# A fused decoder block: first group's values split between the exponentials, and a gate copied out of PSUM by two engines

## The chip, the cores and the metric

The kernel runs on one core of a Trainium2 chip. Five engines work side by side, each on its own list of instructions in a fixed order: PE (matrix multiplication; it reads SBUF and writes PSUM), DVE (vector), ACT (scalar functions and copies), POOL, and SP, which here only issues transfers (DMAs). POOL issues transfers too, on a queue of its own. Semaphores connect the lists: an instruction that waits holds up everything behind it on its engine. The metric is the device time of one execution in microseconds (us). Times of events below are counted from the start of the span.

## The reference

The reference is a whole decoder block over 1024 tokens and 1024 channels in float32: normalization, a chunked retention branch, a dilated-attention branch, sigmoid gates that merge the two, and an MLP. What matters here is the attention branch and its gate:

```python
s = einsum(q, k) * dh**-0.5 + bias
mx = max(s); e = exp(s - mx); den = sum(e)      # per query
p = e / den; lse = mx + log(den)
o = einsum(p, v)
...
wts = softmax(stack(lses))                       # over the 3 groups
att = einsum('gbhs,gbhsd->bshd', wts, o_all)
merged = sigmoid(gate_a) * ret_out + sigmoid(gate_b) * att_out
```

There are three groups of four heads with different windows and dilations. The softmax over the groups mixes the outputs of the groups, head by head.

## The kernel before, in words

Every matrix product is done as three passes: each float32 operand is split into a high part (a rounded copy, made by ACT) and a low part (the rest, made by DVE as `x - hi`), and PE adds low times high, high times low and high times high (`mm3`, L197 to L205).

The program is a list of steps written out by hand. `Steps.run` (L72) goes through it: before a step's body it prepares the weights of the next one or two steps. A weight arrives by one SP transfer of 512 KB into one of three `raw` buffers (L85); `split_w` (L188) makes `raw…h` on ACT and `raw…l` on DVE. As a buffer is used up, the next load is issued on SP.

The attention runs in two passes over pairs of heads (`pair` 0 and 1). The order in a pair is `combos` (L1470): groups 1, 2 and 0, two heads `a` each. Step `att_step(pair, i)` (L1472) projects the keys of `combos[i]` on PE (tile `ak`), and between these matmuls PE computes the scores of `combos[i-1]` (tiles `sc`). DVE adds the bias (tile `P`), takes the row maximum and its negative (`ng`); ACT does the exponentials in place (`scores_end`, L1256). When both heads of group 1 or 2 are done, `stats_out` (L1325) writes their maxima and sums to DRAM (`std`) and reads them back in the order of the tokens (`stn`): two SP transfers, where the second waits for the first to land.

Then come the cover steps (`cover_step`, L1507), which carry one gate projection each on PE (tile `gate`, in one of two PSUM buffers of two banks), as cover for the attention's tail:

- n = 0 computes the scores of the last head of group 0, its exponentials, then `weights(pair)` (L1333): a short chain DVE, ACT (exponential of `wt`, L1346), DVE, which gives the weight of each group. `pscale(0, a)` then scales the probabilities of group 0, blocks shared by DVE (L1367) and ACT (L1369). Only then does ACT do the sigmoid of the first gate out of PSUM (L1538; a table of functions is loaded first), and SP writes it to DRAM.
- n = 1 computes the second gate, and in its middle splits the values of group 0 (`v_split(pair, 0)`, L1297: `vh` on ACT, `vl` on DVE).
- n = 2 begins the products of probabilities and values (`pv`): PE transposes blocks of `P` into PSUM (`pt`, L1384), ACT and DVE split them (`pth` L1388, `ptl` L1389), PE multiplies them with `vl` and `vh` (L1408 to L1410). Between these PE computes the third gate, which takes the PSUM buffer of the first.

The values lie in DRAM (`va_d`). `v_fetch(pair, g)` (L1291) loads them by two SP transfers of 512 KB, cut in rows of 256 numbers (1 KB). For group 0 this is issued at the start of the last key step (`i == len(combos) - 1`). On the list of SP these transfers come after `std` and `stn` of group 2 and after the weight loads of the third and fourth gates.

At the end of the retention, `result_sums` (L574) gives POOL four sums of 2 MB blocks in DRAM, each a copy followed by an accumulating transfer (`dma_sum`, L566 and L567), each of these waiting for the one before it. They run on POOL's queue while the attention of pair 0 begins.

Of the kernel before, what the change touches and what calls it, by code (L numbers as in the profile page):

```python
# [11 lines left out]
F32 = mybir.dt.float32  # L12
F32R = mybir.dt.float32r
AF = mybir.ActivationFunctionType
# [120 lines left out]
def block_kernel(ctx, tc, io, stop=None, dbg=None):  # L135
    nc = tc.nc
    ctx.enter_context(tc.manual_schedule())

    def fv(t):
        return t.bitcast(F32)  # L140
# [350 lines left out]
    def at(gen, n, call):  # L491

        for i, _ in enumerate(gen):
            if i == n:
                call()
            yield

    def drain(gen):
        for _ in gen:
            pass  # L500
# [458 lines left out]
    gate_d = [dram.tile([P, S], F32, name=f"gated{i}") for i in range(16)]  # L959
# [165 lines left out]
    A = {}  # L1125
# [9 lines left out]
    def ring(name, dt=F32R):  # L1135
        return A["p"].tile([P, 1024], dt, tag="ring", bufs=8, name=name)
# [3 lines left out]
    def pslice(g, t, blk):  # L1140

        if g == 0:
            return (t[:, 0:128], 1) if blk == 0 else (t[:, 128 + 256 * (blk - 1):128 + 256 * blk], 2)
        if g == 1:
            r, n = blk // 2, blk % 2
            return (t[:, 384 * r:384 * r + 128], 1) if n == 0 else (t[:, 384 * r + 128:384 * r + 384], 2)
        return t[:, 128 * blk:128 * (blk + 1)], 1
# [108 lines left out]
    def scores_end(pair, g, a):  # L1256
        p, t, st = A["p"], A["P", g, a], A["st"]
        if g == 0:
            nc.vector.reduce_max(st[:, g, 0:1, a], t[:, 0:128], axis=AX.X)
            nc.vector.reduce_max(st[:, g, 1:8, a], t[:, 128:].rearrange("p (b x) -> p b x", b=7), axis=AX.X)  # L1260
        elif g == 1:
            tv = t.rearrange("p (r x) -> p r x", r=4)
            sv = st[:, g].rearrange("p (r n) x -> p r n x", n=2)
            nc.vector.reduce_max(sv[:, :, 0, a], tv[:, :, 0:128], axis=AX.X)
            nc.vector.reduce_max(sv[:, :, 1, a], tv[:, :, 128:384], axis=AX.X)
        else:
            nc.vector.reduce_max(st[:, g, :, a], t.rearrange("p (b x) -> p b x", b=8), axis=AX.X)
        ng = p.tile([P, 8], F32, tag="ng", bufs=2, name=f"ng{pair}{g}{a}")
        nc.vector.tensor_scalar_mul(ng, st[:, g, :, a], -1.0)  # L1269
        for blk in range(8):  # L1270
            v = pslice(g, t, blk)[0]
            nc.scalar.activation(v, v, AF.Exp, bias=ng[:, blk:blk + 1], accum_out=st[:, g, blk, 2 + a:3 + a])  # L1272
# [13 lines left out]
    def v_tile(pair, g, j, n):  # L1286
        if g == 0:
            return A["r1"].tile([P, S], F32R, tag="att", bufs=8, name=f"{n}{pair}{g}{j}")
        return ring(f"{n}{pair}{g}{j}")
# [4 lines left out]
            lo = A["l", g, j] = v_tile(pair, g, j, "vl")  # L1294
            nc.sync.dma_start(fv(lo).rearrange("p (a b) -> p a b", a=4), v_rows(pair, g, j))

    def v_split(pair, g):  # L1297
        for j in range(2):
            lo = A["l", g, j]
            hi = v_tile(pair, g, j, "vh")  # L1300
            nc.scalar.copy(hi, fv(lo))
            nc.vector.tensor_sub(lo, fv(lo), fv(hi))
            A["v", g, j] = (hi, lo)

    def vblk(g, blk, a, i):
        j, b = (blk % 2, blk // 2) if g == 1 else (blk // 4, blk % 4)
# [14 lines left out]
    def blocks(t, g):  # L1321

        return t.rearrange("p (r n) x -> p r n x", n=2) if g == 1 else t
# [9 lines left out]
    def weights(pair):  # L1333

        p, st = A["p"], A["st"]
        stn = [st[:, 0], A["stn"][:, 1], A["stn"][:, 2]]
        mx = p.tile([P, 8, 2], F32, tag="mx", name=f"mx{pair}")
        wt = p.tile([P, 3, 8, 2], F32, tag="wt", name=f"wt{pair}")
        pr = p.tile([P, 3, 8, 2], F32, tag="pr", name=f"pr{pair}")
        sm = p.tile([P, 8, 2], F32, tag="ssum", name=f"ssum{pair}")  # L1340
        wg = p.tile([P, 2, 8, 2], F32, tag="wg", name=f"wg{pair}")
        nc.vector.tensor_max(mx, stn[0][:, :, 0:2], stn[1][:, :, 0:2])
        nc.vector.tensor_max(mx, mx, stn[2][:, :, 0:2])
        for g in range(3):
            nc.vector.tensor_sub(wt[:, g], stn[g][:, :, 0:2], mx)
        nc.scalar.activation(wt, wt, AF.Exp)  # L1346
        for g in range(3):
            nc.vector.tensor_mul(pr[:, g], wt[:, g], stn[g][:, :, 2:4])
        nc.vector.tensor_add(sm, pr[:, 0], pr[:, 1])
        nc.vector.tensor_add(sm, sm, pr[:, 2])  # L1350
        nc.vector.reciprocal(sm, sm)
        for g in range(3):
            nc.vector.tensor_mul(wt[:, g], wt[:, g], sm)
        A["w", 0] = wt[:, 0]
        ds = [dram.tile([S, 2], F32, name=f"wtd{pair}{g}") for g in (1, 2)]
        for g in (1, 2):
            nc.sync.dma_start(natural(ds[g - 1], 0, 2), wt[:, g])
        for g in (1, 2):
            nc.sync.dma_start(blocks(wg[:, g - 1], g), natural(ds[g - 1], g, 2))
            A["w", g] = wg[:, g - 1]  # L1360

    def pscale(g, a):
        t, w = A["P", g, a], A["w", g]
        for blk in range(8):
            v = pslice(g, t, blk)[0]
            if blk in (0, 2, 4, 5, 7):
                nc.vector.tensor_scalar_mul(v, v, w[:, blk, a:a + 1])  # L1367
            else:
                nc.scalar.mul(v, v, w[:, blk, a:a + 1])  # L1369
        A["scaled", g, a] = True  # L1370
# [85 lines left out]
    def weave_pv(main, n, pair, *groups):  # L1456


        parts, waits = sum(4 * len(PT[g]) for g in groups), 2 * len(groups) + 1
        heavy = max(1.0, (parts - waits) / max(1, n - waits))  # L1460
        total = parts + waits * (heavy - 1)
        done = share = 0
        for wait in pv(pair, *groups):
            share += heavy if wait else 1
            while done * total < share * n:
                next(main, None)
                done += 1
        drain(main)

    combos = [(g, a) for g in (1, 2, 0) for a in range(2)]  # L1470

    def att_step(pair, i):  # L1472

        g, a = combos[i]

        def body(*args):
            ps = ps_mm(f"ak{pair}{i}")
            gen = proj_gen(ps, args[-1])
            if i == len(combos) - 1:
                v_fetch(pair, 0)  # L1480
            if i > 0:
                last = combos[i - 1]
                weave(gen, NK, scores_gen(pair, *last), len(SB[last[0]]), lag=2)
            elif pair == 0:
                args[0](1, True)
                for _ in range(4):
                    next(gen)
                on_T(H - 1, NC - 1)
                drain(gen)
                u_final(H - 1)  # L1490
                result_sums()
                open_att()
                args[0](3)
            else:

                weave_pv(at(gen, 0, lambda: v_split(0, 2)), NK - 1, 0, 2)
            if i == 0:
                A["st"] = A["p"].tile([P, 3, 8, 4], F32, tag="st", name=f"st{pair}")
                bias_load(pair)
            k_split(pair, g, a, ps)  # L1500
            if i > 0:
                scores_end(pair, *last)
                if last[1] == 1:
                    stats_out(pair, last[0])
        return body

    def cover_step(pair, n):  # L1507


        i = COVER[pair][n]  # L1510

        def body(*args):
            ps = ps_mm(f"gate0{i}")
            gen = proj_gen(ps, args[-1])
            if n == 0:
                v_fetch(pair, 1)
                weave(gen, 6, scores_gen(pair, *combos[-1]), len(SB[0]), lag=2, rest=False)
                drain(gen)
                scores_end(pair, *combos[-1])
                weights(pair)  # L1520
                for a in range(2):
                    pscale(0, a)
            elif n == 1:
                drain(at(gen, 4, lambda: v_split(pair, 0)))
            elif n == 2:
                v_fetch(pair, 2)

                gen = at(gen, 3, lambda: (args[0](3), v_split(pair, 1)))
                weave_pv(gen, NK - 1, pair, 0)
                for a in range(2):  # L1530
                    pscale(1, a)
            else:
                weave_pv(at(gen, 3, lambda: [pscale(2, a) for a in range(2)]), NK - 1, pair, 1)
            if n > 1:
                t = A["r1"].tile([P, S], F32, tag="att", bufs=8, name=f"g0{i}s")
            else:
                t = ring(f"g0{i}s", F32)
            nc.scalar.activation(t, flat(ps), AF.Sigmoid)  # L1538
            nc.sync.dma_start(gate_d[i], t)
        return body  # L1540

    for pair in range(2):
# [916 lines left out]
```

## Time and profile before

| | |
|---|---|
| median of 3 runs | 2226.19 us (2223.69 to 2228.32) |
| the profiled execution | 2226.56 us, of which the span is 2224.8 us |
| PE busy | 2177.1 us, 98% of the span |
| DVE, ACT, POOL busy | 65%, 41%, 7% of the span |
| transfers | 408.93 MB, mean 184 GB/s |

In the rows of a timeline the first two columns are the start and the busy time in us (of all instructions merged in the row), then engine, line, operation, the tile written and those read, the shape and the count. In brackets stands how long the engine had been idle before it and what ended that. Rows of waits give the engine and line that waited, what for, the total in us, how many times, and the longest. Rows of the transfer queues give packets, MB, and the time that the packets took, as a share of sixteen transfer engines. POOL's queue is `q0 software_dynamic`, SP's is `q1 hardware_dynamic`.

### The profile page before, as it was taken

The numbers are of one execution on the slowest core, as the hardware profiler recorded it, in microseconds if no ns is written. First come the engines' busy times: TensorE is split into PE (matmuls) and PEld (weight loads), VectorE is DVE, ScalarE is ACT, GpSimd is POOL, SyncE is SP. The second block draws the span as 40 slices with busy tenths as digits, with TensorE's granted clock in tenths as the row PEclk, the third lists the DMA queues.
The fourth block names the chain that finished last, engine by engine and source line by source line (L and its number), as shares of the span: only waits on it lengthen the run. The fifth ranks groups of instructions, "written<-read, shape, count | busy, mean of one in ns | idle before, by whom it ended". The sixth has DMA issues, their size and how long they took to land.

```text
span 2224.8 us, 27161 instructions
## 1 busy us (share of the span) xinstructions
PE 2177.1 (98%) x10130; PEld 1803.4 (81%) x10130; DVE 1454.5 (65%) x2285; ACT 907.3 (41%) x1665; POOL 145.5 (7%) x168
## 2 busy tenths in 40 slices
PE   7999999999999999999999999999999999999998
PEld 4888888888877888888888788888778888888887
DVE  6628777764448778855554644676876665787855
ACT  4323332223434445544534633424454445533412
POOL 0001111000012122100000000002100000000003
PEclk9999999999999999999999999999999999999999
DMA  9539999725775556549813355645144444745322
GB/s 364 200 134 284 299 284 284 200 103 189 250 268 169 167 179 212 188 162 248 235 60 96 105 196 211 237 160 176 62 149 152 149 156 168 261 139 171 122 85 77
DMA packets 154371, 408.93 MB, mean 184 GB/s; under 512 B 27062, under 2 KB 54973, under 8 KB 149822
## 3 DMA queue, kind: packets, MB, share of 16 engines
q1 hardware_dynamic: 148542, 363.14, 46.5%
q0 software_dynamic: 5696, 44.04, 8.4%
q8 instruction: 80, 1.31, 0.2%
q14 instruction: 53, 0.43, 0.1%
HBM read 316.27 MB, written 156.13 MB: 212 GB/s over the span
## 4 chain that ended last, share of the span: by engine, by line
PE 86%; DVE 6%; ACT 3%; DMA 2%; issue 1%; POOL 0%; SPq 0%; POOLq 0%; DVEq 0%; ACTq 0%
PE qap L203 5%; PE qap L201 5%; PE qap L205 5%; PE av L769 4%; PE fp L203 4%; PE fp L201 4%; PE fp L205 4%; PE rg L201 2%; PE rg L203 2%; PE rg L205 2%; PE f2a L203 2%; PE f2a L201 2%; PE f2a L205 2%; PE ak L201 2%; PE ak L203 2%; PE ak L205 2%
## 5 line engine op out<-in xcount | busy, mean ns | idle before, releaser
L201 PE MATMUL qap<-hh,qaw 128*128 128x512 f32 x216 | 84.0, 389 | 0.0
L203 PE MATMUL qap<-hl,qaw 128*128 128x512 f32 x216 | 84.0, 389 | 0.0
L205 PE MATMUL qap<-hh,qaw 128*128 128x512 f32 x216 | 84.0, 389 | 0.0
L616 POOL TENSOR_TENSOR j<-qk,j 128x512 fp32r<-128x512 f32 x32 | 43.3, 1352 | 465.0 <-ACT j L615 465.0
L1918 ACT ACTIVATE a<-a 128x512 f32<-128x512 f32 x48 | 30.3, 632 | 76.2 <-DVE a L1917 76.2
L1272 ACT ACTIVATE P<-P,ng 128x128 f32<-128x128 f32 (+1 forms) x96 | 41.9, 438 | 39.2 <-DVE ng L1269 39.2
L258 DVE TENSOR_TENSOR fw<-w1r,fw 128x512 fp32r<-128x512 f32 x48 | 33.0, 688 | 37.6 <-ACT fw L248 37.6
L1815 POOL TENSOR_TENSOR accnf<-accnf,sqnf 128x256 f32<-128x256 f32 (+1 forms) x18 | 16.6, 922 | 613.5 <-ACT sqnf L1814 613.4
L258 DVE TENSOR_TENSOR qaw<-wa,qaw 128x512 fp32r<-128x512 f32 x54 | 36.0, 685 | 30.9 <-ACT qaw L248 30.9
L2104 ACT CAST w2h<-w2s 128x512 fp32r<-128x512 f32 x36 | 22.4, 621 | 78.1 <-DVE w2s L2142 77.0
L201 PE MATMUL fp<-h2h,fw 128*128 128x512 f32 x128 | 50.0, 390 | 0.0
L203 PE MATMUL fp<-h2l,fw 128*128 128x512 f32 x128 | 49.8, 389 | 0.0
L205 PE MATMUL fp<-h2h,fw 128*128 128x512 f32 x128 | 49.8, 389 | 0.0
L201 PE MATMUL roa<-rh,rwl 128*128 128x512 f32 x128 | 49.8, 389 | 0.0
L203 PE MATMUL roa<-rl,rwh 128*128 128x512 f32 x128 | 49.8, 389 | 0.0
L205 PE MATMUL roa<-rh,rwh 128*128 128x512 f32 x128 | 49.8, 389 | 0.0
L1653 DVE TENSOR_TENSOR rwl<-rwl,rwh 128x1024 fp32r<-128x1024 f32 x25 | 30.2, 1221 | 29.1 <-ACT rwh L1683 29.1
L638 ACT COPY sm<-sT 128x128 f32<-128x128 f32 x32 | 8.5, 266 | 98.8 <-PE sT L629 92.7
L201 PEld LDWEIGHTS qap<-hh,qaw 128*128 128x128 f32 x216 | 40.5, 188 | 8.5
L205 PEld LDWEIGHTS qap<-hh,qaw 128*128 128x128 f32 x216 | 40.5, 188 | 8.4
L203 PEld LDWEIGHTS qap<-hl,qaw 128*128 128x128 f32 x216 | 40.5, 188 | 8.4
L1815 POOL TENSOR_TENSOR accn<-accn,sqn 128x512 f32<-128x512 f32 x12 | 15.5, 1294 | 478.5 <-ACT sqn L1814 478.5
(3081 smaller groups left out, 7181.0 us busy)
## 6 DMA issues: line engine op xcount, KB each, us to landing
v<-vd SPq DMA_DIRECT2D x32, 512.0 KB, 4.9
raw<-in_w_ada_dram SPq DMA_DIRECT2D x32, 512.0 KB, 4.9
w1r<-in_w_ff_dram SPq DMA_DIRECT2D x32, 512.0 KB, 5.0
vd<-vo SPq DMA_DIRECT2D x24, 512.0 KB, 6.5
yt<-y POOLq DMA_DIRECT2D x6, 2048.0 KB, 15.3
xsd<-as SPq DMA_DIRECT2D x24, 512.0 KB, 2.7
w2r<-in_w_ff2s_dram SPq DMA_DIRECT2D x24, 512.0 KB, 7.6
em<-in_w_ada_dram SPq DMA_DIRECT2D x16, 512.0 KB, 10.2
```

Source lines behind the costliest of these rows:

```text
L201: nc.tensor.matmul(o, wl, xh, start=first, stop=False, skip_group_check=skip)
L203: nc.tensor.matmul(o, wh, xl, start=False, stop=False, skip_group_check=skip)
L205: nc.tensor.matmul(o, wh, xh, start=False, stop=last, skip_group_check=skip)
L258: nc.vector.tensor_sub(t[:, 512:], src, fv(t[:, :512]))
L616: nc.gpsimd.tensor_sub(t[:, 1], src, fv(t[:, 0]))
L638: nc.scalar.copy(sm, ps[:, :C])
L769: nc.tensor.matmul(av[g][c], x[k][:, c * C:(c + 1) * C], w[j][:, ws], start=k == 0 and (x, j) == parts[0], stop=k == NK - 1 and (x, j) == ...
L1272: nc.scalar.activation(v, v, AF.Exp, bias=ng[:, blk:blk + 1], accum_out=st[:, g, blk, 2 + a:3 + a])
L1653: nc.vector.tensor_sub(lo, fv(lo), fv(hi))
L1815: (nc.vector if f == 7 else nc.gpsimd).tensor_add(G["acc", key], G["acc", key], sq)
L1918: nc.scalar.activation(o, o, AF.Relu)
L2104: nc.scalar.copy(hi, src)
```

## The change

The change has these parts, for each of the two pairs:

1. `v_fetch(pair, 0)` is issued one key step earlier (`len(combos) - 2`). On SP's list its two transfers now stand ahead of `std` and `stn` of group 2 and of the loads of the third and fourth gates.
2. The high parts `vh` of group 0 are made on ACT in step n = 0, between the exponentials of the two heads of group 0, instead of in step n = 1.
3. The low parts `vl` are made on DVE inside `weights`, while ACT does the last exponentials and that of `wt`.
4. The first gate is copied out of PSUM after `pscale`: its first half by DVE, its second by ACT. Its sigmoid is done in place in step n = 1, after that of the second gate, and so is its write to DRAM; the table load moves with it.

```diff
-    def v_split(pair, g):
+    def v_split(pair, g, low=True):
         for j in range(2):
             lo = A["l", g, j]
             hi = v_tile(pair, g, j, "vh")
             nc.scalar.copy(hi, fv(lo))
-            nc.vector.tensor_sub(lo, fv(lo), fv(hi))
             A["v", g, j] = (hi, lo)
+            if low:
+                v_low_part(g, j)
+
+    def v_low_part(g, j):
+        hi, lo = A["v", g, j]
+        nc.vector.tensor_sub(lo, fv(lo), fv(hi))
...
         nc.scalar.activation(wt, wt, AF.Exp)
+
+        for j in range(2):
+            v_low_part(0, j)
...
-            if i == len(combos) - 1:
+            if i == len(combos) - 2:
                 v_fetch(pair, 0)
...
                 drain(gen)
+                v_split(pair, 0, False)
                 scores_end(pair, *combos[-1])
                 weights(pair)
                 for a in range(2):
                     pscale(0, a)
+
+                t = ring(f"g0{i}s", F32)
+                nc.vector.tensor_copy(t[:, :512], ps[:, 0])
+                nc.scalar.copy(t[:, 512:], ps[:, 1])
             elif n == 1:
-                drain(at(gen, 4, lambda: v_split(pair, 0)))
+                drain(gen)
...
+            if n == 0:
+                A["gate"] = i, t
+                return
...
             nc.scalar.activation(t, flat(ps), AF.Sigmoid)
             nc.sync.dma_start(gate_d[i], t)
+            if n == 1:
+                i0, t0 = A["gate"]
+                nc.scalar.activation(t0, t0, AF.Sigmoid)
+                nc.sync.dma_start(gate_d[i0], t0)
```

## The prediction

> **What bounds the kernel now.** I read the page first, then the waits and the timeline of PE around the changed steps, then ACT and DVE in the same stretch, and last SP's list, the transfer queues and POOL.
>
> ```profile
> span 2224.8 us, 27161 instructions
> PE 2177.1 (98%) x10130; PEld 1803.4 (81%) x10130; DVE 1454.5 (65%) x2285; ACT 907.3 (41%) x1665; POOL 145.5 (7%) x168
> ```
>
> PE is busy for all but 48 us of the span, and the matmuls are the same after the change. So only PE's idle gaps count, those that close and those that open. Pair 0, PE:
>
> ```profile
> 1079.51 0.60 PE L1384 MATMUL pt000(0, 0, 0)_8939<-ct,P 128*128 128x128 f32 x4
> 1080.89 0.73 PE L201 MATMUL gate<-hh,raw_8603l 128*128 128x512 f32 x2 [0.79 <-ACT g00s L1538]
> 1085.96 0.38 PE L1409 MATMUL pv<-ptl000(0, 0, 0)_8945,vh 128*128 128x256 f32 x1 [0.45 <-DVE ptl000(0, 0, 0)_8945 L1389]
> ```
>
> Pair 1, from the waits of PE:
>
> ```profile
> PE gate L201 <- ACT g04s L1538: 0.8, 1, 0.8
> PE pv L1409 <- DVE ptl100(0, 0, 0)_10284 L1389: 0.5, 1, 0.5
> ```
>
> The third gate waits until ACT has emptied the first gate's PSUM buffer, and the first value products wait until DVE has the low part of the transposed probabilities. Pair 1 repeats pair 0. Behind these waits stand ACT and DVE:
>
> ```profile
> 1063.52 1.03 ACT L191 CAST raw_8603h<-raw 128x1024 fp32r<-128x1024 f32 x1
> 1070.62 0.40 ACT L1272 ACTIVATE P<-P,ng 128x128 f32<-128x128 f32 x1 [6.07 <-DVE ng L1269]
> 1075.99 2.51 ACT L1369 ACTIVATE P<-P,wt 128x256 f32<-128x256 f32 x6 [1.30 <-DVE wt L1353]
> 1078.52 1.28 ACT L1538 ACT_TABLE_LOAD   x1
> 1079.82 1.02 ACT L1538 ACTIVATE g00s<-gate 128x1024 f32<-128x1024 f32 x1
> 1080.74 1.04 ACT L191 CAST raw_8609h<-raw 128x1024 fp32r<-128x1024 f32 x1
> 1081.67 2.00 ACT L1301 CAST vh<-vl 128x1024 fp32r<-128x1024 f32 x2
> 1083.57 1.03 ACT L1538 ACTIVATE g01s<-gate 128x1024 f32<-128x1024 f32 x1
> 1084.48 0.58 ACT L1388 CAST pth000(0, 0, 0)_8944<-pt000(0, 0, 0)_8939 128x512 fp32r<-128x512 f32 x1
> ```
>
> ```profile
> 1064.58 1.23 DVE L192 TENSOR_TENSOR raw_8603l<-raw,raw_8603h 128x1024 fp32r<-128x1024 f32 x1 [4.95 <-ACT raw_8603h L191]
> 1074.72 0.18 DVE L1348 TENSOR_TENSOR pr<-wt,st 128x16 f32<-128x16 f32 x1 [3.47 <-ACT wt L1346]
> 1082.95 2.35 DVE L1302 TENSOR_TENSOR vl<-vl,vh 128x1024 fp32r<-128x1024 f32 x2
> 1085.22 0.68 DVE L1389 TENSOR_TENSOR ptl000(0, 0, 0)_8945<-pt000(0, 0, 0)_8939,pth000(0, 0, 0)_8944 128x512 fp32r<-128x512 f32 x1
> ```
>
> From 1075.99 to 1085 ACT has no idle time, and the splits of the values stand right ahead of what PE waits for. Note also 1063.52: the split of the third gate's weight stands on ACT and on DVE ahead of the whole chain of the last head of group 0.
>
> **Parts 2 to 4: what they gain.** The high parts (2.00 us on ACT) move into ACT's idle 6.07 us before 1070.62, where they end by 1066.6, if the values have landed. The low parts (2.35 us on DVE) move into the 3.47 us in which DVE waits for ACT, from 1071.25 to 1073.6, so `pr` at 1074.72 isn't late. Both cost nothing there; that cover is the chain of exponentials. For the half copies the nearest rows are copies of the same shape out of PSUM:
>
> ```profile
> L775 ACT COPY avo<-av 128x512 f32<-128x512 f32 x24 | 13.3, 601 | 33.9 <-PE av L769 31.1 <-DMA vad<-avo 1.7
> L703 DVE COPY state<-kv 128x512 f32<-128x512 f32 x8 | 5.4, 689 | 2.9 <-PE kv L205 2.9
> ```
>
> The scalings end at 78.5 (1075.99 + 2.51; I write the last two digits of 10xx). ACT's half copy ends at 79.1, DVE's at 79.25. PE is through with `pt000` at 80.1, so the third gate starts there instead of at 80.89: the 0.79 us are gone. ACT goes on with `raw_8609h` (0.93 from start to start) to 80.05, the table load to 81.33, two sigmoids of 0.91 from start to start (1083.57 to 1084.48) to 83.15, and `pth000` starts there instead of at 84.48. DVE is no longer held by the low parts (82.95 + 2.35 = 85.3, where `ptl000` stood), so `ptl000` follows `pth000` at about 83.9, not 85.22. PE's L1409 then starts at about 84.65 instead of 85.96: **1.3 us a pair**, 2.6 us in all; the 0.79 is part of it. Bounds: 0.8 (only the buffer wait goes) and 1.6 (all gaps go) a pair. The added sigmoid's write to DRAM on SP, one place later, has no reader in this stretch: nothing.
>
> **Part 1: the earlier fetch, on SP's queue.** Here I expect the time to be lost, in pair 0 alone.
>
> ```profile
> 1028.95 12.10 SPq L85 DMA_DIRECT2D raw<-in_w_gate_dram  x2
> 1048.07 0.33 SPq L1330 DMA_DIRECT2D std<-st  x1
> 1058.23 0.38 SPq L1331 DMA_DIRECT2D stn<-std  x1
> 1058.69 1.08 SPq L85 DMA_DIRECT2D raw<-in_w_gate_dram  x2
> 1060.30 1.01 SPq L1295 DMA_DIRECT2D vl<-vad  x2
> ```
>
> ```profile
> 1045.96 1.16 POOL L567 DMA_DIRECT2D yt<-y  x1 [20.60 <-DMA yt<-yt]
> 1060.30 0.52 POOL L566 DMA_DIRECT2D yt<-yt  x1 [13.19 <-DMA yt<-y]
> 1072.11 1.15 POOL L567 DMA_DIRECT2D yt<-y  x1 [11.28 <-DMA yt<-yt]
> ```
>
> The fetch moves from 1060.30 to right behind the first two gate loads, that is to 1041, ahead of `std`, `stn` and the third gate's load (1058.69, the weight that ACT splits at 1063.52). SP waits at `stn` for `std` to land: 10 us here, for 16 KB. In pair 1 the same pair of rows is 1.8 us apart:
>
> ```profile
> 1206.48 0.33 SPq L1330 DMA_DIRECT2D std<-st  x1
> 1208.27 0.38 SPq L1331 DMA_DIRECT2D stn<-std  x1
> ```
>
> The difference is POOL's sums, which fill the transfer engines from 1046 to 1060 (an accumulate) and on to 1072 (a copy). Queues in 1030 to 1040 (another accumulate runs), then SP's queue in 1215.4 to 1217.4 (pair 1, values alone), then POOL's in 1064 to 1071 (the copy):
>
> ```profile
> q0 software_dynamic: 238, 2.74, 105.3%
> q1 hardware_dynamic: 196, 0.00, 2.8%
> q1 hardware_dynamic: 723, 0.75, 106.3%
> q0 software_dynamic: 47, 2.10, 72.3%
> ```
>
> In the first window SP's queue got one packet through for each of POOL's, however small: 196 against 238, some 20 to 24 a microsecond. Alone, packets of values go at 360 a microsecond. And the queue is served in order: the second gate's weight, issued by 1041.05, was there at
>
> ```profile
> 1050.10 1.05 ACT L191 CAST raw_8501h<-raw 128x1024 fp32r<-128x1024 f32 x1 [0.17 <-DMA raw<-in_w_gate_dram]
> ```
>
> The values' 1024 packets (1 MB in rows of 1 KB) come behind that weight. From 1050 to the end of the accumulate at 1060 they get 10 x 24 = 240 through; the other 784 need 784 / 360 = 2.2 us, to 1062.2. Only then `std`'s packets pass, so `stn` is issued at about 1062.6 instead of 1058.23, and the third gate's load at 1063.1. Before, that load took at most 4.8 us (58.69 to 63.52); it would be there at 67.9. But the copy's large packets (2.10 MB in 47, over 40 KB each) are on the engines from 1064 to about 1071, and SP's queue gets one packet per turn. So most of the 512 KB wait until 1071 and take 1.4 us more (0.75 MB in 2 us): **the split starts at about 1072.9 instead of 1063.52, 9.4 us late**. Bounds: 4.4 us late (it passes ahead of the copy) and 11 (it begins only when the copy has landed, near 1072, and takes 2.5).
>
> What is queued behind the split: on ACT the moved high parts, the last exponentials, `wt`, the scalings; on DVE the bias adds of the last head, its maximum, `weights`. From 1063.52 to 1078.5 that chain waits for nothing but itself, so all moves by 9.4. The first transposes had up to 3 us of slack on PE (75.99 plus half a microsecond against 79.51), and the gate copies and `ptl000` have less than 1. PE's L1409 comes at 84.65 + 9.4 = 94.05 instead of 85.96: **pair 0 loses 8.1 us**. In pair 1 POOL is through, the values are fetched well before, and the 1.3 us are gained.
>
> PE stands idle for some 6 us at 1079.5. After shorter gaps this kernel's PE got half its clock:
>
> ```profile
> core 0: us, PE busy (x) PEld busy (x) DVE busy (x) ACT busy (x) POOL busy (x), PEclk, DMA share, GB/s
> 665.00:668.40 3.40, 3.40 (x13) 2.92 (x12) 0.00 (x0) 0.27 (x1) 0.00 (x0) 0.50 0.79 270
> ```
>
> 3.4 us at half cost 1.7 us of work. Here PE has 3.5 us of work up to the first value product and would then wait over a microsecond for `pth000` and `ptl000`, so most of it is hidden: I take 0.3, between 0 and 2. The Trainium skill ("TensorE: Matmul & The Clock Gate", Part 1) says the clock drops after an idle window of about 3.4 us; the row agrees in length.
>
> **The sum.** -1.3 (pair 1) + 8.1 (pair 0) + 0.3 = +7.1 us. Against the profiled execution's 2226.56 (1.8 around the span of 2224.8) that is 2233.7. That execution lies 0.4 above the median, so 2233.3 against the median; I say 2233.5.
>
> **Rivals.**
> - *The fetch is hidden* and pair 0 gains like pair 1: -2.6, 2223.7. For it: before, nothing waited for `stn`, and DVE and ACT have slack of 5 and 6 us just ahead of the chain, but behind the split of the weight, not before it. It needs the third gate's weight by 1063.5; from 2.6 us late on, the change as a whole loses. Against it: the packet counts.
> - *Late, but ahead of the copy*: 4.4 - 2.6 = +1.8, 2228.2. It needs the load through within a microsecond or two of 1063.1, or a copy that starts later.
> - *More than one packet of SP's queue per turn.* With four of the 1 KB pieces per turn, 960 of 1024 would pass by 1060, `stn` would follow at about 1060.6, the weight at 1065.9: 2.4 late, a net of -0.2, 2226.2. The count of 196 against 238 speaks against it, but is of 16-byte pieces. The Trainium skill ("DMA: Bandwidth & Descriptors", "Queues, rings and completion order") has an engine drain "a whole packet" of several descriptors before it switches; by that rule this rival would hold, and the trace's count disagrees.
> - *Worse*: the clock stays at half through the value products, or the second sum's last accumulate catches the load as well: +12 to +15, 2238 to 2241.
>
> **How the numbers follow.** Forecast 62% (own range 2231 to 2237, from 7.2 to 11 us late with 0 to 2 for the clock); hidden 12%, late but ahead of the copy 10%, several pieces per turn 8%, worse 8%. 0.2% of this time is 4.5 us, about what a measurement of this kernel can tell from no change. Slower by more than that: forecast and worse, 70%. Within it: 27%, the three others less 3% for a hidden fetch where gaps behind the changed steps close as well. Range 2224.5 to 2238: it takes in the bounds and leaves out about 2 in 10, the best of the hidden fetch and the worst case.
>
> **What the profile after would show.** In pair 0: `vl` of group 0 issued near 1041, `stn` of group 2 past 1062, DVE and ACT idle until a DMA brings the third gate's weight near 1073, PE idle 5 to 7 us ahead of `pt000`, half clock around it. In pair 1: no wait for the first gate, L1409 1.3 us earlier. Wrong would be: `stn` still near 1058, or the weight there by 1066.

## The result and the profile after

| | before | after |
|---|---|---|
| median | 2226.28 us (2223.69 to 2228.32, 4 runs) | 2236.54 us (2235.09 to 2237.51, 4 runs) |
| span of the profiled execution | 2224.8 us | 2233.2 us |
| ratio of the times | | 1.0045, 95% interval 1.0033 to 1.0057 |

The changed kernel is slower by 10 us. PE's work is the same; its waits are not. Waits of PE in the changed kernel, first around the change in pair 0, then in pair 1 (engine, line, tile, what it waited for, total us, times, longest):

```profile
PE pt000(0, 0, 0)_8941 L1392 <- DVE P L1375: 6.5, 1, 6.5
PE gate L201 <- ACT g00s L1535: 2.3, 1, 2.3
...
PE pv L1416 <- ACT pth100(0, 0, 0)_10287 L1396: 0.8, 1, 0.8
...
PE pv L1417 <- DVE ptl100(0, 0, 0)_10288 L1397: 0.3, 1, 0.3
```

In pair 0 there is a new wait of 6.5 us ahead of the first transposes, and the wait for the first gate's buffer, which was to go, has grown from 0.8 to 2.3. SP's list shows where this begins (start, us taken, line, transfer):

```profile
1027.87 11.45 SPq L85 DMA_DIRECT2D raw<-in_w_gate_dram  x2
1039.37 4.32 SPq L1295 DMA_DIRECT2D vl<-vad  x2
1046.78 0.33 SPq L1335 DMA_DIRECT2D std<-st  x1
1061.61 0.36 SPq L1336 DMA_DIRECT2D stn<-std  x1
1062.08 7.13 SPq L85 DMA_DIRECT2D raw<-in_w_gate_dram  x2
```

The values now stand ahead of the statistics. `std` takes from 1046.78 to 1061.61 to land, 14.8 us instead of 10.2, and the load of the third gate's weight can only be issued then. ACT and DVE wait for it:

```profile
1071.99 1.05 ACT L191 CAST raw_8607h<-raw 128x1024 fp32r<-128x1024 f32 x1 [9.68 <-DMA raw<-in_w_gate_dram]
1072.95 2.00 ACT L1301 CAST vh<-vl 128x1024 fp32r<-128x1024 f32 x2
1079.11 0.40 ACT L1272 ACTIVATE P<-P,ng 128x128 f32<-128x128 f32 x1 [4.17 <-DVE ng L1269]
1084.47 2.51 ACT L1377 ACTIVATE P<-P,wt 128x256 f32<-128x256 f32 x6 [1.30 <-DVE wt L1361]
1087.68 0.58 ACT L1535 COPY g00s<-gate 128x512 f32<-128x512 f32 x1 [0.70 <-DVE g00s L1534]
1092.39 0.58 ACT L1396 CAST pth000(0, 0, 0)_8946<-pt000(0, 0, 0)_8941 128x512 fp32r<-128x512 f32 x1
```

```profile
1073.07 1.23 DVE L192 TENSOR_TENSOR raw_8607l<-raw,raw_8607h 128x1024 fp32r<-128x1024 f32 x1 [14.74 <-ACT raw_8607h L191]
1079.66 2.35 DVE L1308 TENSOR_TENSOR vl<-vl,vh 128x1024 fp32r<-128x1024 f32 x2
1086.96 0.68 DVE L1534 COPY g00s<-gate 128x512 f32<-128x512 f32 x1
```

The weight's split starts at 1071.99 instead of 1063.52, and this execution was 1.3 us ahead of the earlier one up to there (below), so it is 9.8 us late. Everything behind it keeps its old distances: 12.47 us from the split to the scalings before (1063.52 to 1075.99), 12.48 after. The moved splits of the values lie in the idle time that was foreseen for them. The row at 1087.68 was not foreseen: ACT's half of the gate copy waits 0.70 us for DVE's half.

PE in pair 0, with the last matmul ahead of the wait:

```profile
1077.76 0.61 PE L205 MATMUL gate<-hh,raw_8501h 128*128 128x512 f32 x2
1084.90 1.09 PE L1392 MATMUL pt000(0, 0, 0)_8941<-ct,P 128*128 128x128 f32 x4 [6.53 <-DVE P L1375]
1088.32 1.22 PE L201 MATMUL gate<-hh,raw_8607l 128*128 128x512 f32 x2 [2.33 <-ACT g00s L1535]
1094.70 0.28 PE L1416 MATMUL pv<-pth000(0, 0, 0)_8946,vl 128*128 128x256 f32 x1
1094.81 0.28 PE L1417 MATMUL pv<-ptl000(0, 0, 0)_8947,vh 128*128 128x256 f32 x1
```

A pair of gate matmuls takes 0.46 from start to start, so `pt000` was due at 1078.22, 1.29 earlier than in the execution before. From there to L1417 are 16.6 us; before, from 1079.51 to 1085.96, it was 6.45: pair 0 loses 10.1. In pair 1 the same stretch is now 5.76, 6.46 before: it gains 0.7. The first two rows are from before, the last two from after:

```profile
1237.91 0.60 PE L1384 MATMUL pt100(0, 0, 0)_10278<-ct,P 128*128 128x128 f32 x4
1244.37 0.39 PE L1409 MATMUL pv<-ptl100(0, 0, 0)_10284,vh 128*128 128x256 f32 x1 [0.45 <-DVE ptl100(0, 0, 0)_10284 L1389]
...
1246.69 0.60 PE L1392 MATMUL pt100(0, 0, 0)_10282<-ct,P 128*128 128x128 f32 x4
1252.45 0.38 PE L1417 MATMUL pv<-ptl100(0, 0, 0)_10288,vh 128*128 128x256 f32 x1 [0.34 <-DVE ptl100(0, 0, 0)_10288 L1397]
```

10.1 - 0.7 - 1.3 (shorter ahead of the change) gives +8.1, next to the 8.4 by which the spans differ. The 1.3 lies in this one profiled execution; without it the two pairs account for 9.4 us of the 10 us between the medians.

### The profile page after: what moved, and what is told of

It is laid out like the page before. It is cut to its first block, busy times and chain, and to the rows that moved or that the text cites. A ratio compares the mean times of both kernels' runs of the same rounds, so it can differ in the third digit from the quotient of the medians.

```text
span 2233.2 us, 27170 instructions
## 1 busy us (share of the span) xinstructions
PE 2179.3 (98%) x10130; PEld 1806.2 (81%) x10130; DVE 1456.3 (65%) x2287; ACT 908.1 (41%) x1667; POOL 145.3 (7%) x168
## 4 chain that ended last, share of the span: by engine, by line
PE 85%; DVE 6%; DMA 5%; ACT 3%; issue 1%; POOL 0%; SPq 0%; POOLq 0%; DVEq 0%; ACTq 0%
PE qap L201 5%; PE qap L205 5%; PE qap L203 5%; PE av L769 4%; PE fp L203 4%; PE fp L201 4%; PE fp L205 4%; PE rg L203 2%; PE rg L201 2%; PE rg L205 2%; PE f2a L203 2%; PE f2a L205 2%; PE f2a L201 2%; PE ak L201 2%; PE ak L203 2%; PE ak L205 2%
## 5 line engine op out<-in xcount | busy, mean ns | idle before, releaser
L1835 POOL TENSOR_TENSOR accnf<-accnf,sqnf 128x256 f32<-128x256 f32 (+1 forms) x18 | 16.6, 921 | 613.9 <-ACT sqnf L1834 613.9
## 6 DMA issues: line engine op xcount, KB each, us to landing
em<-in_w_ada_dram SPq DMA_DIRECT2D x16, 512.0 KB, 10.2
```

What stands on the lines that cost most here:

```text
L1835: (nc.vector if f == 7 else nc.gpsimd).tensor_add(G["acc", key], G["acc", key], sq)
```

## The experiments

Two theories stood against each other: the **queue theory** of the prediction (the fetch ahead of the statistics on SP's queue, slowed by POOL's sums, makes the third gate's weight late) and the rival that the **rearranged work on ACT and DVE** costs the time. The first four kernels ran together, with the kernel before at 2225.83 us, and so did the last four, with the kernel before at 2227.04.

### Part 1 alone, and all but part 1

The first kernel is the one before with

```diff
-            if i == len(combos) - 1:
+            if i == len(combos) - 2:
                 v_fetch(pair, 0)
```

> The kernel before with part 1 alone: the values of group 0 are fetched one key step earlier, everything else as before. Queue theory (the fetch stands on SP's queue ahead of the statistics and of the third gate's weight, and POOL's sums slow it): the third gate's weight is split near 1073 instead of 1063.5, PE loses some 9.7 us in pair 0 and nothing in pair 1, half clock costs up to 2 more: 9 to 12 us slower than before, about 2236 to 2238. Rival (the loss comes from the order of the splits and of the gate copy on ACT and DVE): no change, within 1 us of before.

Measured: 2236.91 us against 2225.83, ratio 1.0056 (1.0039 to 1.0072). The whole loss comes with this one line. ACT's wait and PE's rows, pair 0 and pair 1:

```profile
1070.25 1.05 ACT L191 CAST raw_8607h<-raw 128x1024 fp32r<-128x1024 f32 x1 [9.37 <-DMA raw<-in_w_gate_dram]
```

```profile
1083.16 1.09 PE L1384 MATMUL pt000(0, 0, 0)_8939<-ct,P 128*128 128x128 f32 x4 [6.22 <-DVE P L1367]
1093.59 0.28 PE L1409 MATMUL pv<-ptl000(0, 0, 0)_8945,vh 128*128 128x256 f32 x1
...
1245.47 0.60 PE L1384 MATMUL pt100(0, 0, 0)_10278<-ct,P 128*128 128x128 f32 x4
1251.92 0.39 PE L1409 MATMUL pv<-ptl100(0, 0, 0)_10284,vh 128*128 128x256 f32 x1 [0.45 <-DVE ptl100(0, 0, 0)_10284 L1389]
```

PE's last gate pair started at 1076.33, so by the same 0.46 `pt000` was due at 1076.79; to L1409 these are 16.8 us, 10.3 more than before. Pair 1 takes 6.45 us as it did: there POOL's sums are over, and the fetch does no harm.

The second kernel is the changed one with that line put back.

> The changed kernel with part 1 undone: the fetch stands where it was before, parts 2 to 4 stay. Queue theory: stn is back at 1058 and the third gate's weight at 1063.5, but the values land only near 1073.9, so the high parts hold up ACT: last exponentials of pair 0 at about 1075 instead of 1070.6, some 4.3 us late, less 0.7 gained behind; pair 1 gains 0.7: 2 to 4 us slower than before. Rival (the loss comes from parts 2 to 4): still 8 us or more slower, with the weight of the third gate in time.

Measured: 2229.61 us, ratio 1.0015 (1.0006 to 1.0024): 3.3 us by the ratio, 3.8 by the medians, inside the 2 to 4 that the queue theory gave. The weight is in time again (split at 1061.09, with no wait), but the values are not:

```profile
1070.28 1.05 ACT L1301 CAST vh<-vl 128x1024 fp32r<-128x1024 f32 x1 [8.16 <-DMA vl<-vad]
1071.76 1.05 ACT L1301 CAST vh<-vl 128x1024 fp32r<-128x1024 f32 x1 [0.43 <-DMA vl<-vad]
```

So part 2 needs part 1 in this place: with POOL's sums running, the values are either late for ACT or they make the weight late.

### POOL's sums moved by their place in the program

In both kernels the call went from the end of the retention to the start of pair 1:

```diff
                 u_final(H - 1)
-                result_sums()
...
             else:
+                result_sums()
                 weave_pv(at(gen, 0, lambda: v_split(0, 2)), NK - 1, 0, 2)
```

> The changed kernel with POOL's four sums issued at the start of pair 1 instead of at the end of the retention. Queue theory: pair 0 then looks like pair 1, std and stn 2 us apart, the third gate's weight in time, no half clock; both pairs gain 0.7: 1 to 2 us faster than before, about 2224.5, and 10 faster than the changed kernel. Rival (the place on SP's queue costs by itself, without POOL): still 5 us or more slower than before.

> The kernel before with the four sums issued at the start of pair 1: the control for the run above. Both theories: within 1.5 us of before, as nothing on PE waited for a transfer in pair 0; std and stn of group 2 some 2 us apart instead of 10. If it is 2 us or more faster, the sums cost before too, by a way that I have not seen.

Measured: 2236.05 us (ratio 1.0051, 1.0036 to 1.0066) and 2226.78 us (1.0008, 0.9999 to 1.0017). Neither theory was tested, as the sums did not move. POOL in the first of the two:

```profile
1045.87 1.16 POOL L567 DMA_DIRECT2D yt<-y  x1 [19.98 <-DMA yt<-yt]
1062.54 0.52 POOL L566 DMA_DIRECT2D yt<-yt  x1 [15.52 <-DMA yt<-y]
```

That is where they were (1044.75 and 1060.96 in the changed kernel). From 989 on POOL's rows hold only these sums, and its list waits only for the transfers that they read, so in these two runs the place of the call made no difference. The two runs are repeats of the two kernels, and show how far they repeat.

### POOL's sums held by something that waits

Here the call is taken from the end of the retention as above, a small product on POOL reads the group weights of pair 0, and the sums stand behind it:

```diff
                 u_final(H - 1)
-                result_sums()
...
             else:
+                hold = A["p"].tile([P, 8, 2], F32, tag="hold", name="hold")
+                nc.gpsimd.tensor_tensor(hold, A["w", 2], A["w", 2], op=ALU.mult)
+                result_sums()
                 weave_pv(at(gen, 0, lambda: v_split(0, 2)), NK - 1, 0, 2)
```

> The changed kernel with POOL held, by a small product that reads the group weights of pair 0, so that its four sums start only in pair 1. In the runs before, moving the call alone moved nothing, since POOL's list held nothing that waits. Queue theory: in pair 0 std and stn of group 2 are some 2 us apart, the third gate's weight is split by 1064, no wait of several us ahead of pt000, no half clock in pair 0; both pairs gain 0.7: 1 to 2 us faster than before, about 2224.5. Rival (the place on SP's queue costs by itself, the 1 MB ahead of the statistics): the weight is 3 us or more late even without POOL, and the kernel 1 us or more slower than before.

> The kernel before with the four sums held to pair 1 in the same way: the control. Both theories: within 1 us of before, since no instruction on PE waits for these transfers. If it is faster by 1 us or more, that much of the gain of the run above is not the change's.

Measured: the changed kernel 2224.51 us, ratio to the kernel before 0.9991 (0.9982 to 1.0); the control 2225.47, 0.9994 (0.9985 to 1.0003). With the same place on SP's queue, but without the sums beside it, the loss of 10 us is gone. POOL and SP in the first of the two:

```profile
1084.29 0.22 POOL L1503 TENSOR_TENSOR hold<-wg 128x16 f32<-128x16 f32 x1 [113.79 <-DMA wg<-wtd]
```

```profile
1045.69 0.33 SPq L1335 DMA_DIRECT2D std<-st  x1
1047.12 0.36 SPq L1336 DMA_DIRECT2D stn<-std  x1
```

`std` lands in 1.4 us, and the third gate's weight is split at 1061.13 with no wait. From `pt000` to L1417 PE takes 5.78 us, a gain of 0.67, in pair 0 as in pair 1. The control came out 1.3 us faster than the kernel before by its ratio, 1.6 by the medians; its interval takes in no difference, but by the expectation that much of this gain may not be the change's. Against the control the changed kernel gains 1.0 us by the medians, where the rows give twice 0.67, and the intervals overlap. These runs take both delays away at once, the accumulate's ahead of `stn` and the copy's behind it; no run separates them, and how much each costs is read from rows (below).

### The gate copied by one engine

```diff
-                nc.vector.tensor_copy(t[:, :512], ps[:, 0])
-                nc.scalar.copy(t[:, 512:], ps[:, 1])
+                nc.vector.tensor_copy(t, flat(ps))
```

This on top of the held sums:

> As the first of these runs, with the first gate copied out of PSUM by DVE alone, both halves in one instruction. Theory (ACT's half waits for DVE's half, as both write one tile, and this 0.7 us is what a pair gained less than predicted): ACT goes from the scalings straight to the weight's split, pth of the first block starts 1.2 us earlier than in the changed kernel, the waits of PE for the gate and for pth and ptl of the first block go: 1.4 to 1.6 us a pair, about 3 us faster than before, 2223. Rival (the copy in two halves is the better one): no more gain than the first of these runs, or PE waits for the gate's buffer, as DVE needs 1.2 us for the whole.

Measured: 2222.17 us, ratio to the kernel before 0.9978 (0.9969 to 0.9987). ACT, DVE and PE in pair 0:

```profile
1074.51 2.51 ACT L1377 ACTIVATE P<-P,wt 128x256 f32<-128x256 f32 x6 [1.31 <-DVE wt L1361]
1076.92 1.03 ACT L191 CAST raw_8605h<-raw 128x1024 fp32r<-128x1024 f32 x1
1081.14 0.58 ACT L1396 CAST pth000(0, 0, 0)_8937<-pt000(0, 0, 0)_8932 128x512 fp32r<-128x512 f32 x1
```

```profile
1076.99 1.23 DVE L1535 COPY g00s<-gate 128x1024 f32<-128x1024 f32 x1
```

```profile
1078.01 0.60 PE L1392 MATMUL pt000(0, 0, 0)_8932<-ct,P 128*128 128x128 f32 x4
1082.49 0.39 PE L1417 MATMUL pv<-ptl000(0, 0, 0)_8938,vh 128*128 128x256 f32 x1
```

DVE's copy of the whole gate ends at 78.2, when PE is still at the transposes. ACT has no copy at all and no wait in front of the weight's split; `pth` starts 6.63 us after the scalings instead of 7.92 (changed kernel). PE's rows print no idle time in this stretch: 4.48 us instead of 6.45, in both pairs. That is 2.0 us a pair, more than the 1.4 to 1.6 expected, which was the sum of the idle times printed before. These say too little, as matmuls overlap: `pt000` is busy for 0.60 us, but without a wait the gate's first matmul starts 0.36 us after it (1078.01 to 1078.37). Before, it started 1.38 us after it (1079.51 to 1080.89), so 1.02 us go where 0.79 of idle time were printed. By medians the kernel is 4.9 us faster than the kernel before and 3.3 faster than the control with the held sums; the rows give 4.0.

The last kernel leaves the sums where they were and keeps the old fetch and split in pair 0:

```diff
-            if i == len(combos) - 2:
+            if i == len(combos) - 1 - pair:
                 v_fetch(pair, 0)
...
-                v_split(pair, 0, False)
+                if pair:
+                    v_split(pair, 0, False)
...
-                nc.vector.tensor_copy(t[:, :512], ps[:, 0])
-                nc.scalar.copy(t[:, 512:], ps[:, 1])
+                nc.vector.tensor_copy(t, flat(ps))
```

(with `v_low_part` in `weights` for pair 1 alone, and the split of pair 0 in the middle of the second gate).

> The sums where they were; the earlier fetch and the split between the exponentials in pair 1 alone, and the gate copied by DVE alone in both pairs. Queue theory: pair 0 has the third gate's weight at 1063.5 as before and gains 0 to 0.3; pair 1 gains 1.4 to 1.6: 1.4 to 1.9 us faster than before, about 2224.5. Rival (pair 0's loss has a part that does not come from the fetch): pair 0 still loses 1 us or more.

Measured: 2224.94 us, ratio 0.9988 (0.9979 to 0.9997). PE, pair 0 and pair 1:

```profile
1078.98 0.60 PE L1392 MATMUL pt000(0, 0, 0)_8940<-ct,P 128*128 128x128 f32 x4
1085.35 0.39 PE L1417 MATMUL pv<-ptl000(0, 0, 0)_8946,vh 128*128 128x256 f32 x1 [0.34 <-DVE ptl000(0, 0, 0)_8946 L1397]
...
1237.32 0.60 PE L1392 MATMUL pt100(0, 0, 0)_10280<-ct,P 128*128 128x128 f32 x4
1241.80 0.38 PE L1417 MATMUL pv<-ptl100(0, 0, 0)_10286,vh 128*128 128x256 f32 x1
```

Pair 0 gains 0.1 (6.37 us), pair 1 2.0 (4.48). Nothing is left of pair 0's loss. As this kernel leaves out the moved splits of pair 0 together with its fetch, it clears the gate copy alone; that the fetch brings the loss rests on the first kernel.

## Why the prediction was right, and where it was off

- **Which part loses, where, and by what**: right. Part 1 alone brings the loss, in pair 0 alone, and it goes with POOL's sums.
- **How late the weight is**: 9.4 us predicted, 9.8 measured, in two delays. The first was to hold `stn` until 1062.6; counted on the clock of the execution before, it was issued at 1061.61 + 1.29 = 62.9, so 4.7 us late. The second, POOL's copy, was to add 5.0. From `stn` to the split it took 10.38 us (1061.61 to 1071.99) instead of 5.29 (1058.23 to 1063.52), so 5.1 more. But neither came about quite as written, and that both sizes came out so close is in part luck. I had 240 of the values' packets pass beside the accumulate and the rest after it, and only the weight's packets behind the copy. These are the transfer queues of the changed kernel: all packets in 1045.3 to 1049.3; in 1050 to 1058 all packets, then by queue; POOL's queue in 1061.5 to 1067, where SP's has no packet; and SP's in 1067 to 1069:

```profile
DMA packets 1026, 1.54 MB, mean 385 GB/s; under 512 B 44, under 2 KB 858, under 8 KB 1022
...
DMA packets 368, 1.76 MB, mean 220 GB/s; under 512 B 82, under 2 KB 165, under 8 KB 165
q0 software_dynamic: 202, 1.65, 99.1%
q1 hardware_dynamic: 165, 0.09, 5.6%
...
q0 software_dynamic: 32, 2.10, 103.1%
...
q1 hardware_dynamic: 1040, 0.02, 29.2%
```

  In the first 4 us 814 of the values' 1024 packets of 1 KB passed (858 under 2 KB less 44 under 512 B), before the accumulate's packets were there in number. But their tail and `std` behind it did not: in the next 8 us only 165 of SP's packets passed beside 202 of POOL's. `std` lands with the last of its packets, so it landed when the accumulate was over, as predicted, with far fewer packets in front of it than I had counted. During the copy SP's queue got nothing, as predicted, but it came back within 1067 to 1069 and not at 1071 - 1.29 = 1069.7. What then passed were 1040 tiny packets, the 16 KB of `stn`, for which I had counted no time; only behind them came the weight.

  That SP's queue gets about one packet for each of POOL's fits the kernel before best, where `std` had SP's queue to itself in 1052 to 1056: 100 packets beside 104. For pieces of 1 KB the rows show fewer than one a turn, 165 in all beside 202, and nothing of the several a turn that the rival had. The Trainium skill ("DMA: Bandwidth & Descriptors", "Queues, rings and completion order") has an engine drain a whole packet of several descriptors from one queue before it switches; if a packet of these rows is one descriptor, which they don't say, that is not what they show.
- **The gain of parts 2 to 4**: 1.3 us a pair predicted, 0.7 measured in pair 1. The step that failed is "ACT's half copy ends at 79.1, DVE's at 79.25": they don't run side by side, as ACT's waits for DVE's (0.70 us idle). With one copy on DVE, ACT's wait and copy go, and the pair gains 2.0. That the wait comes from both writing one tile is argued, not shown: both halves also read one PSUM tile, and no run gave them two. The upper bound of 1.6 a pair was too low as well, as it added up printed idle times.
- **The clock**: the step was right and its size too small. I took 0.3 us, between 0 and 2. PE ran at half clock for 10 us, not 3.4. In rows of this kind the second figure behind the stretch is PE's busy time, and PEclk is the third from the end:

```profile
1083.70:1087.10 3.40, 1.09 (x4) 0.72 (x4) 3.32 (x16) 2.51 (x6) 0.00 (x0) 0.50 1.02 298
1087.10:1090.50 3.40, 2.18 (x5) 1.80 (x6) 1.77 (x2) 2.80 (x3) 0.00 (x0) 0.50 0.68 118
1090.50:1094.00 3.50, 3.50 (x13) 2.95 (x13) 1.00 (x2) 3.43 (x6) 0.00 (x0) 0.50 0.00 0
```

  I had half clock end after 3.4 us. It went on through two such stretches in which PE waited for part of the time, and ended with the first in which PE was busy throughout. In the kernel with part 1 alone it was the same (1.09, 1.06 and 3.40 us busy in three stretches of 3.4 us from 1081.9 on). The row in the prediction, 3.40 us at 0.50, stood behind a wait of 2.21 us, so it showed how long half clock can last and not which idle time sets it off.

  The work between `pt000` and the first value product took 7.5 us without its wait (1084.90 to 1094.70, less 2.33) instead of 4.5 (1079.51 to 1085.12, less 0.79 and 0.32). At full clock PE would have waited for `ptl000`, which ends at 1093.69 (1093.00 + 0.69), so by the rows L1417 could start near 1093.75, not 1094.81: about 1.1 us.
- **The sum**: pair 0 was to lose 8.1 + 0.3. With 0.4 more for the weight, 0.65 for the copies in a row and 0.8 more for the clock this is 10.25; measured 10.1. With pair 1's 0.7 the change costs 9.4 us where 7.1 were predicted. All three misses add to the loss, which is why the median lies in the upper part of the range.

## What to carry to other kernels

A transfer moved ahead in a list is paid for by what it is moved past: ask which load behind it stands in front of a chain, and what other queue fills the transfer engines just then. Transfers in small pieces suffer here, since beside the accumulate SP's queue got no more packets through than POOL's (100 beside 104, 165 beside 202), though its packets were far smaller: the 16 KB of `std`, for which SP waits, landed in 1.4 us without the sums, in 10.2 beside them, and in 14.8 with the values ahead as well. And two engines that copy halves of one tile into one tile took turns here rather than share the work, so look for the wait between them before counting on the half.

## What was not expected of the hardware

- After an idle time of 6.5 us PE had half its clock for 10 us, though it had work for 6.8 of them. The kernel without part 1, with waits of 1.3 and 2.7 us, had half clock for 3.4 us there (from 1081.5). Its clock was full again by 1084.9, and yet the mean was 0.62 in a stretch of continuous work some 60 us later:

```profile
1142.00:1146.00 4.00, 4.00 (x19) 3.42 (x19) 2.67 (x2) 0.40 (x1) 0.00 (x0) 0.62 0.00 0
```

  The last wait of PE before this was one of 0.88 us at 1140.44, in a stretch of 3.4 us (1139.6 to 1143) with PE busy for 2.56. What sets it off there is left open.
- Moving the call of POOL's sums in the program did not move its transfers: 1045.87 against 1044.75 us for the same row. A small product with a late input, put ahead of them on POOL's list, did: the first sum then started behind it, at 1084.90.
